# A two-layer token backbone on one core: lower parts of the output projection on GpSimd, an overflow flag computed behind the first gather, two weight splits behind the router's scores, and a later estimate of the experts' transfers

## The chip, the cores and the metric

The kernel runs on one core of one Trainium2 chip. The core has a matrix engine (TensorE, PE in the profile), a vector engine (VectorE, DVE), an activation engine (ScalarE, ACT), GpSimd (POOL), and SyncE (SP), which here issues most transfers. All weights lie in the chip's main memory and are brought in by DMA. The metric is device time in microseconds (us), lower is better. The kernel before has a median of 1495.08 us over three runs (1493.68 to 1499.86).

## The reference, cut to what matters

The input is 256 latent tokens of 1024 values and 256 context tokens. Two layers follow each other; each is a token mixer and then a mixture of experts, both added to the stream, and a last RMS norm. All arithmetic is float32.

```python
for i in range(2):
    hx = rmsnorm(x, mix_norm_g[i]) * (1 + sc1) + sh1
    yx = rglru_mixer(...) if i == 0 else sgu_mixer(...)   # ends in an output projection (... @ w_out)
    x = x + g1 * yx
    hx = rmsnorm(x, ffn_norm_g[i]) * (1 + sc2) + sh2
    x = x + g2 * moe_ffn(hx, ...)

def moe_ffn(xn, ...):
    scores = sigmoid(xn @ router_w)                       # 64 experts
    ... # 4 of 8 groups of experts are kept, then the top 8 experts of each token
    gate = chosen scores / their sum * 2.5
    # each chosen expert: (silu(x @ w_gu[:, :256]) * (x @ w_gu[:, 256:])) @ w_down, times its gate
    return routed + swiglu(xn, ws_gu, ws_down)            # and one shared expert for all tokens
```

Layer 0's mixer is a recurrent block: input projection, gates, a linear scan in both directions over five heads of 256, and the output projection `a_w_out` (1280 x 1024). Layer 1's is a gated MLP.

## The kernel before, in words

**Order of work.** The program writes the order of each engine's instructions by hand (a manual schedule): an engine does its instructions in the order in which the Python code issues them, and waits where an operand is not there yet. Layer 0's mixer takes the span from 0 to about 248 us, its experts to about 787, layer 1's mixer to about 948 and its experts to about 1487.

**Float32 by three products.** TensorE multiplies such operands in a shorter format, so a weight and an activation are each split in an upper part and a lower part, and `mm3` makes three products (upper by upper, upper by lower, lower by upper). Activations' parts are `zh`, `zl`, `hh`, `hl`, `fh`, `fl`; weights' are `wh`, `wl`. The weights are split by `splitter`: ScalarE casts a piece into `wh` (L564), and another engine subtracts it from the piece into `wl` (L565); which one, the caller's function `eng(i, c)` says for tile i and piece c. Calling the splitter's `get(q)` issues casts and subtractions up to two pieces ahead of piece q.

**Layer 0's mixer.** Its weight tiles of 1 MB are split in pieces of 128x1024 (two per tile). The output projection has four tiles O0 to O3 and a tile Q; they are multiplied while the last heads' scans run on VectorE. `split_eng` (L707) gives O0 to GpSimd, and of O1, O2 and O3 the first piece to GpSimd and the second to VectorE; Q's two pieces go to VectorE. `ready(n)` (L716) asks the splitter for pieces up to n; `B(h, q)`, the gates of head h, calls it once for each of its two halves jt (L838), ahead of the activations L841 and L842.

**Experts.** At the start of a layer's experts, `rstd_of` takes a root (ScalarE, L532) and VectorE's L533 to L535 finish it; the router's scores (L1270, a tanh L1271) follow, then the choice of experts on VectorE, counts on TensorE behind the mask `mb` (L1325), and a list `order` of the 64 experts by load (L1358). SyncE then starts their transfers, in that order. Each expert has three tiles of 1 MB: two of `m_gu` (gate and up) and one of `m_dn`. They stream through a ring of 12 slots (`wr`, `wx`); class `Stream` issues a tile's transfer (L382) when a slot has come free. Tokens are gathered by a product with a 0/1 matrix `S` (`gather`, bank `b<-S,xt`, into `xg`), multiplied by `gate_up` (GU, `b<-wr,xg` and `b<-wx,xg`), turned (`flip`), multiplied by `down` (DN, `b<-wr,ht`), and scattered back.

**Work that is always there.** The shared expert, two fixed experts and five of the heaviest ones are computed for all 256 tokens by `over_all` (steps of `s<-hh,wh`: here called up-steps, six products of 128x256 in a half step) and `all_down` (`b<-fh,wh`: down-steps, 24 products). They wait in a list `ups`; the planner places them. `up(n)` issues n of them; `until(tiles)` issues them as long as it believes that the next expert's tile has not arrived:

```python
st.now = st.dma = max(st.now, st.dma)                # L1361, when order is known
self.dma = max(self.dma, self.since.get(w, 0.0)) + LOAD   # LOAD, LATE = 2.6, -0.3
self.due.append(self.dma + LATE)                     # in pump(), for each transfer
if t <= st.now: break                                # until(): t is the tile's due time
```

`st.now` is the planner's own clock, moved on by fixed costs of each step. Before the root L532, `over_all` of the shared expert issues the splits of its first four pieces (the cast L564 on ScalarE, the subtraction on GpSimd); only then does `up(1)` return and `rstd_of` follow.

**Overflow flag.** A general path handles an input in which an expert gets more tokens than its slots. A flag says whether it is needed: `cape` and `over` on VectorE (L1418, L1420), a product of 1x1 on TensorE (L1423), a cast on VectorE (L1424). `overflow()` makes the engines load the flag (L1428) and branch; it stands after `gather(0, 0)` and `gather(0, 1)` in the program. In this data the path is not taken.

Of the kernel before, what the change touches and what calls it, by code (L numbers as in the profile page):

```python
# [10 lines left out]
F32 = mybir.dt.float32  # L11
F32R = mybir.dt.float32r
BF = mybir.dt.bfloat16
I32 = mybir.dt.int32
AF = mybir.ActivationFunctionType
OP = mybir.AluOpType

P = 128
# [211 lines left out]
LOAD, LATE = 2.6, -0.3  # L230
COST = dict(step=1.46, down2=2.95, half=3.6, side=0.6, scatter=4.0, flip=0.25, gather=2.0, down=3.6)
# [70 lines left out]
def _body(nc, tc, a, pp, rp, ps, ps1, dr):  # L302
    V, S, G, PE = nc.vector, nc.scalar, nc.gpsimd, nc.tensor
    st = Stream(nc)

    def mm(out, lhsT, rhs, start, stop):
        PE.matmul(out, lhsT, rhs, start=start, stop=stop, skip_group_check=True)  # L307
# [7 lines left out]
    def bank(shape=(P, 512)):  # L315
        return ps.tile(list(shape), F32, name="b")
# [321 lines left out]
    def mixer0(rx):  # L638
      with tc.tile_pool(name="m0", bufs=1) as mp, tc.tile_pool(name="m0t", bufs=2) as tp:
# [67 lines left out]
        def split_eng(i, c):  # L707
            kind, j = plan0[users[i]]
            return G if (kind, j) in (("A", 0), ("O", 0)) or kind == "O" and c == 0 else V
# [5 lines left out]
        def ready(n):  # L715

            wq(n - 3)
# [93 lines left out]
        def B(h, q):  # L811
# [4 lines left out]
            for jt in range(2):  # L816
# [21 lines left out]
                ready(q + 7 + jt)  # L838
# [310 lines left out]
    def moe(l, tail):  # L1149
      rsb = bank()  # L1150
      with tc.tile_pool(name=f"e{l}", bufs=1) as mp, tc.tile_pool(name=f"e{l}t", bufs=2) as tp:
# [33 lines left out]
        def lower(i, c):  # L1185
            return V if c % 2 else G

        def over_all(ns, gate=None, eng=None):

            wq = splitter(tp, ns, eng or lower, 5)  # L1190
            p, out, at = [], [], []
# [28 lines left out]
            ups.append((lambda: wq(-1 if eng is None else 1), ns[0], 0.0, None))  # L1220
# [37 lines left out]
        prev = (over_all(sgu, eng=lambda i, c: G if i == 0 else lower(i, c)), sdn)  # L1258
# [12 lines left out]
        S.activation(out=sc, in_=sc, func=AF.Tanh, scale=0.5)  # L1271
        spread()
# [88 lines left out]
        st.now = st.dma = max(st.now, st.dma)  # L1361
# [54 lines left out]

        cape = mp.tile([P, 1], F32, name="cape")
        V.scalar_tensor_tensor(out=junk[:, :64], in0=pb[:, :64], scalar=1.0, in1=C["cap"], op0=OP.mult, op1=OP.mult, accum_out=cape)  # L1418
        over = mp.tile([P, 1], F32, name="over")
        V.tensor_tensor(out=over, in0=nc_, in1=cape, op=OP.is_gt)  # L1420
        pf = bank()
        mm(pf[0:1, 0:1], over[0:64, :], onesf[0:64, 0:1], True, True)
        flag = mp.tile([1, 1], I32, name="flag")  # L1423
        V.tensor_copy(out=flag, in_=pf[0:1, 0:1])  # L1424

# [145 lines left out]
        def spend(what):  # L1571
            st.now += COST[what]

# [3 lines left out]
        spend("gather")  # L1577
        overflow()
# [89 lines left out]
```

## Time and profile before

| | us |
|---|---|
| median of three runs | 1495.08 (1493.68 to 1499.86) |
| the profiled execution's own time | 1495.63 |
| its span, first to last instruction | 1493.5 |
| PE busy | 1401.8 (94%) |
| DVE busy | 757.3 (51%) |
| ACT busy | 517.7 (35%) |
| POOL busy | 325.4 (22%) |

The mean granted TensorE clock over the span is 0.977. The chain that ended last is 49% PE, 23% issue, 5% POOL, 3% DVE and 1% ACT. Of the chip's transfers the span moved 514.85 MB, at a mean of 345 GB/s. A busy share is a mean over stretches with different limits, so the timeline of each stretch says more: there a row gives the start, the time, engine, line, operation, the tile written and the tiles read, how many instructions it sums up, and in brackets the engine's idle time ahead of it with the instruction that ended it.

### The profile page before, as it was taken

Reading aid. Unit: us, or ns where it says so; the run is one execution under the profiler, and the core shown is the slowest. Engines: PE = TensorE matmul, PEld = TensorE weight load, DVE = VectorE, ACT = ScalarE, POOL = GpSimd, SP = SyncE. Lnnn points to the kernel's source line nnn. Section 1 sums busy time; section 2 is a strip of 40 time slices with the busy share of each in tenths; the row PEclk is TensorE's granted clock in tenths of the full one; section 3 lists DMA queues with packets and bytes.
Section 4 is the critical chain, followed back from the end, with each engine's and each line's share of the span. In section 5 each row is a group of like instructions: output and inputs, shape, how many; then the busy total and the mean of one; then the engine's idle time right before and its main releaser. Section 6 shows DMA issues by size and latency. Waiting matters only on the chain.

```text
span 1493.5 us, 27187 instructions
## 1 busy us (share of the span) xinstructions
PE 1401.8 (94%) x10752; PEld 978.8 (66%) x10752; DVE 757.3 (51%) x1378; ACT 517.7 (35%) x874; POOL 325.4 (22%) x412
## 2 busy tenths in 40 slices
PE   6899997998989999999999999889899999999997
PEld 4677776646556575666657899656556667566664
DVE  6689996514254333334446786533425334343534
ACT  4777883311123122222325445511212222212222
POOL 1300033410222212212101441421303222211210
PEclk9999999999999999999999999999999999999999
DMA  9766695598999999999999744469798999999994
GB/s 375 310 267 246 240 384 206 205 380 329 378 384 376 421 420 420 421 419 420 420 418 379 273 169 159 153 235 402 319 390 323 417 419 421 420 420 420 421 421 188
DMA packets 77443, 514.85 MB, mean 345 GB/s; under 512 B 9856, under 2 KB 10240, under 8 KB 17024
## 3 DMA queue, kind: packets, MB, share of 16 engines
q1 hardware_dynamic: 74720, 508.91, 84.2%
q10 hardware_dynamic: 2592, 4.16, 0.9%
q8 instruction: 86, 1.41, 0.4%
q14 instruction: 45, 0.37, 0.1%
HBM read 511.99 MB, written 1.05 MB: 344 GB/s over the span
## 4 chain that ended last, share of the span: by engine, by line
PE 49%; issue 23%; POOL 5%; DVE 3%; ACT 1%; ACTq 0%; POOLq 0%; DVEq 0%
PE b L307 42%; PE s L307 7%; POOL wl L565 2%; POOL S L1396 2%; PE b L1532 1%; DVE wl L565 1%; DVE h L990 0%; POOL Y L1281 0%; ACT wh L564 0%; DVE v L1109 0%; POOL hl L1286 0%; DVE v L1046 0%; DVE xt L1411 0%; DVE u L998 0%; ACT Y L1282 0%
## 5 line engine op out<-in xcount | busy, mean ns | idle before, releaser
L307 PE MATMUL b<-wr,xg 128*32 128x512 f32 (+2 forms) x1464 | 292.8, 599 | 4.8 <-DMA wr<-in_m_gu 3.2
L565 POOL TENSOR_TENSOR wl<-wr,wh 128x512 fp32r<-128x512 f32 (+1 forms) x67 | 98.4, 1480 | 605.4 <-ACT wh L564 573.3
L307 PE MATMUL b<-wx,xg 128*32 128x512 f32 (+2 forms) x744 | 199.4, 599 | 3.3 <-DMA wx<-in_m_gu 3.3
L565 DVE TENSOR_TENSOR wl<-wr,wh 128x512 fp32r<-128x512 f32 (+1 forms) x155 | 146.4, 971 | 50.8 <-ACT wh L564 49.8
L564 ACT CAST wh<-wr 128x512 fp32r<-128x512 f32 (+1 forms) x222 | 143.1, 684 | 74.5 <-PE b L307 46.6
L1157 DVE SCALAR_TENSOR_TENSOR xT<-b,mod,xT 128x256 f32<-128x256 f32 x304 | 130.3, 478 | 74.2 <-PE b L307 68.3
L1525 DVE TENSOR_TENSOR h<-h,b 128x256 f32<-128x256 f32 x44 | 18.5, 420 | 274.3 <-ACT h L1524 274.3
L307 PEld LDWEIGHTS b<-wr,xg 128*32 128x32 f32 (+2 forms) x1464 | 79.1, 118 | 118.3 <-issue 103.7
L1524 ACT ACTIVATE h<-b 128x256 f32<-128x256 f32 x44 | 16.9, 384 | 396.4 <-PE b L307 396.4
L307 PE MATMUL s<-hh,wh 128*128 128x256 f32 x512 | 151.1, 295 | 2.4 <-ACT wh L564 2.4
L307 PE MATMUL b<-wr,ht 128*32 128x512 f32 (+2 forms) x752 | 146.8, 597 | 1.6 <-ACT ht L1534 1.6
L307 PE MATMUL s<-hh,wl 128*128 128x256 f32 x512 | 144.1, 281 | 1.8 <-POOL wl L565 1.7
L1548 DVE SCALAR_TENSOR_TENSOR Y<-b,gt,Y 128x512 fp32r<-128x512 f32 x88 | 65.9, 750 | 154.1 <-ACT Y L1547 154.1
L307 PE MATMUL s<-hl,wh 128*128 128x256 f32 x512 | 143.6, 280 | 0.0
L565 POOL TENSOR_TENSOR wl<-wx,wh 128x512 fp32r<-128x512 f32 (+1 forms) x48 | 69.0, 1455 | 327.3 <-ACT wh L564 260.4
L307 PEld LDWEIGHTS s<-hh,wh 128*128 128x128 f32 x512 | 97.1, 190 | 30.1 <-issue 26.7
L1547 ACT ACTIVATE Y<-b,gt 128x512 fp32r<-128x512 f32 x88 | 60.4, 688 | 142.0 <-PE b L307 135.7
L307 PE MATMUL b<-wx,ht 128*32 128x512 f32 (+2 forms) x352 | 103.2, 599 | 1.3 <-DMA wx<-in_m_dn 0.8
L307 PEld LDWEIGHTS s<-hh,wl 128*128 128x128 f32 x512 | 97.0, 190 | 2.4 <-POOL wl L565 2.1
L1396 POOL TENSOR_SCALAR S<-cst,agq 128x32 fp32r<-128x32 f32 (+3 forms) x208 | 84.1, 429 | 66.1 <-PE b L307 51.0
L307 PEld LDWEIGHTS s<-hl,wh 128*128 128x128 f32 x512 | 97.3, 190 | 0.4
L307 PEld LDWEIGHTS b<-wx,xg 128*32 128x32 f32 (+2 forms) x744 | 50.2, 117 | 70.9 <-issue 60.1
(283 smaller groups left out, 2806.8 us busy)
## 6 DMA issues: line engine op xcount, KB each, us to landing
wr<-in_m_gu SPq DMA_DIRECT2D x174, 1024.0 KB, 12.9
wx<-in_m_gu SPq DMA_DIRECT2D x82, 1024.0 KB, 11.9
wr<-in_m_dn SPq DMA_DIRECT2D x81, 1024.0 KB, 11.9
wx<-in_m_dn SPq DMA_DIRECT2D x41, 1024.0 KB, 11.1
wr<-in_ada_w SPq DMA_DIRECT2D x32, 1024.0 KB, 9.1
wr<-in_a_in SPq DMA_DIRECT2D x10, 1024.0 KB, 8.1
wr<-in_ada SPq DMA_DIRECT2D x8, 1024.0 KB, 12.2
wr<-in_ada_h SPq DMA_DIRECT2D x6, 1024.0 KB, 5.1
```

The costliest lines, as they stand in the source:

```text
L307: PE.matmul(out, lhsT, rhs, start=start, stop=stop, skip_group_check=True)
L564: S.copy(out=hi, in_=t)
L565: eng(i, c).tensor_tensor(out=lo, in0=t, in1=hi.bitcast(F32), op=OP.subtract)
L1157: V.scalar_tensor_tensor(out=xT[:, d, :], in0=y, scalar=mod[:, l, 5, d:d + 1], in1=xT[:, d, :], op0=OP.mult, op1=OP.add)
L1396: (G if b else V).tensor_scalar(out=s[:, tt, i * P + o:i * P + o + wd], in0=C["iota1"][:, j:j + wd], scalar1=agq[:, tt, q:q + 1], scalar2= ...
L1524: S.activation(out=h, in_=p[:, :256], func=AF.Silu)
L1525: V.tensor_tensor(out=h, in0=h, in1=p[:, 256:], op=OP.mult)
L1532: PE.transpose(p[:, k * P:(k + 1) * P], h[:, k * P:(k + 1) * P], ident)
L1547: S.activation(out=hi, in_=p, func=AF.Copy, scale=gts[g])
L1548: V.scalar_tensor_tensor(out=y[:, 1, 512 * c:512 * c + 512], in0=p, scalar=gts[g], in1=hi.bitcast(F32), op0=OP.mult, op1=OP.subtract)
```

## The change

Four edits, in all of which the same things are computed.

1. `split_eng` gives every piece of O0 to O3 to GpSimd; and for head 4's second half (jt = 1) `ready` asks for two pieces more, ahead of L841.
2. Of the four pieces of the shared expert that are split ahead of the root, two stay there; the other two are issued by `more()`, behind the scores' tanh.
3. When `order` is known the planner's estimate of the transfers' start is set `ORDER` = 4.0 us behind its clock.
4. The flag's four instructions are issued behind the two gathers, still ahead of `overflow()`.

Two lines come in at the top, so a line of the kernel after is 2 (from L706 on 2, from L1189 on 4, behind L1271 up to 11) higher than before.

```diff
@@ -228,6 +228,8 @@
 
 
 LOAD, LATE = 2.6, -0.3
+
+ORDER = 4.0
 COST = dict(step=1.46, down2=2.95, half=3.6, side=0.6, scatter=4.0, flip=0.25, gather=2.0, down=3.6)
 
 READY = 5.0
@@ -706,7 +708,7 @@
 
         def split_eng(i, c):
             kind, j = plan0[users[i]]
-            return G if (kind, j) in (("A", 0), ("O", 0)) or kind == "O" and c == 0 else V
+            return G if (kind, j) == ("A", 0) or kind == "O" else V
 
 
         base = 8
@@ -835,7 +837,7 @@
                         p = pg[2 * g + d]
                         S.activation(out=(ta, ti)[g][:, d, :], in_=p, func=AF.Tanh, scale=0.5, bias=(rb_, ib_)[g][:, d, ft:ft + 1])
 
-                ready(q + 7 + jt)
+                ready(q + 7 + (3 if jt and h == 4 else jt))
                 for d in range(2):
                     n1, n2 = nz[:, d, ft:ft + 1], nz2[:, d, ft:ft + 1]
                     S.activation(out=te[:, d, :], in_=ta[:, d, :], func=AF.Tanh, scale=n1, bias=n1)
@@ -1185,9 +1187,11 @@
         def lower(i, c):
             return V if c % 2 else G
 
-        def over_all(ns, gate=None, eng=None):
+        def over_all(ns, gate=None, eng=None, early=None):
 
             wq = splitter(tp, ns, eng or lower, 5)
+            if early is not None:
+                early.append(wq)
             p, out, at = [], [], []
 
             def step(k, x):
@@ -1217,7 +1221,7 @@
                 V.tensor_tensor(out=lo, in0=fv, in1=hi.bitcast(F32), op=OP.subtract)
                 out.extend((hi, lo))
 
-            ups.append((lambda: wq(-1 if eng is None else 1), ns[0], 0.0, None))
+            ups.append((lambda: wq(-1), ns[0], 0.0, None))
             ups.extend([(lambda k=k, x=x: step(k, x), ns[min(k + 2, 7) // 4], COST["step"] / 2, None) for k in range(8) for x in range(2)])
             return out, at
 
@@ -1255,7 +1259,12 @@
         ngu = [[st.reserve("n_gu") for _ in range(2)] for _ in range(NAT)]
         sdn = st.reserve("s_dn")
         ndn = [st.reserve("n_dn") for _ in range(NAT)]
-        prev = (over_all(sgu, eng=lambda i, c: G if i == 0 else lower(i, c)), sdn)
+        early = []
+        prev = (over_all(sgu, eng=lambda i, c: G if i == 0 else lower(i, c), early=early), sdn)
+
+        def more():
+            early[0](1)
+
         for e in range(NAT):
             f = over_all(ngu[e], ident[:, 64 + e:65 + e])
             all_down(*prev)
@@ -1269,6 +1278,7 @@
         for tt in range(2):
             V.scalar_tensor_tensor(out=sc[:, tt, :], in0=tail.rt[:, tt, :], scalar=rstd[:, tt:tt + 1], in1=tail.csh, op0=OP.mult, op1=OP.add)
         S.activation(out=sc, in_=sc, func=AF.Tanh, scale=0.5)
+        more()
         spread()
         if l:
             for i in range(2, 4):
@@ -1358,7 +1368,8 @@
         V.tensor_scalar(out=order, in0=po[0:1, 0:64], scalar1=float(64 * l), scalar2=None, op0=OP.add)
         orders[l] = order
         st.ready.add(("order", l))
-        st.now = st.dma = max(st.now, st.dma)
+        st.now = max(st.now, st.dma)
+        st.dma = st.now + ORDER
         st.pump()
         V.tensor_scalar(out=sc, in0=sc, scalar1=0.5, scalar2=0.5, op0=OP.mult, op1=OP.add)
         V.tensor_copy(out=nc_, in_=ncol)
@@ -1413,16 +1424,6 @@
         up(9)
         if l:
             ada_half_done(5, ada_p, tp, "hf", 1)
-
-        cape = mp.tile([P, 1], F32, name="cape")
-        V.scalar_tensor_tensor(out=junk[:, :64], in0=pb[:, :64], scalar=1.0, in1=C["cap"], op0=OP.mult, op1=OP.mult, accum_out=cape)
-        over = mp.tile([P, 1], F32, name="over")
-        V.tensor_tensor(out=over, in0=nc_, in1=cape, op=OP.is_gt)
-        pf = bank()
-        mm(pf[0:1, 0:1], over[0:64, :], onesf[0:64, 0:1], True, True)
-        flag = mp.tile([1, 1], I32, name="flag")
-        V.tensor_copy(out=flag, in_=pf[0:1, 0:1])
-
 
         def overflow():
             fv = nc.values_load(flag[0:1, 0:1], min_val=0, max_val=64)
@@ -1575,6 +1576,16 @@
         gather(0, 1)
         spend("gather")
         spend("gather")
+
+        cape = mp.tile([P, 1], F32, name="cape")
+        V.scalar_tensor_tensor(out=junk[:, :64], in0=pb[:, :64], scalar=1.0, in1=C["cap"], op0=OP.mult, op1=OP.mult, accum_out=cape)
+        over = mp.tile([P, 1], F32, name="over")
+        V.tensor_tensor(out=over, in0=nc_, in1=cape, op=OP.is_gt)
+        pf = bank()
+        mm(pf[0:1, 0:1], over[0:64, :], onesf[0:64, 0:1], True, True)
+        flag = mp.tile([1, 1], I32, name="flag")
+        V.tensor_copy(out=flag, in_=pf[0:1, 0:1])
+
         overflow()
         for b in range(NB):
             if b + 1 < NB:
```

On GpSimd, at the output projection of layer 0 (`wr6` is the slot of O0, `wr5` of O1, `wx0` of O2, `wx1` of O3), before:

```order
L565 TENSOR_TENSOR wl_1755<-wr6_1683,wh_1754 128x1024
L565 TENSOR_TENSOR wl_1827<-wr6_1683,wh_1826 128x1024
L565 TENSOR_TENSOR wl_1911<-wr5_1693,wh_1910 128x1024
L565 TENSOR_TENSOR wl_1982<-wx0_1766,wh_1981 128x1024
L565 TENSOR_TENSOR wl_2065<-wx1_1768,wh_2064 128x1024
L619 TENSOR_TENSOR hf_2195<-hf_2195 128x256
```

And after:

```order
L567 TENSOR_TENSOR wl_1755<-wr6_1683,wh_1754 128x1024
L567 TENSOR_TENSOR wl_1827<-wr6_1683,wh_1826 128x1024
L567 TENSOR_TENSOR wl_1875<-wr5_1693,wh_1874 128x1024
L567 TENSOR_TENSOR wl_1915<-wr5_1693,wh_1914 128x1024
L567 TENSOR_TENSOR wl_1982<-wx0_1766,wh_1981 128x1024
L567 TENSOR_TENSOR wl_1986<-wx0_1766,wh_1985 128x1024
L567 TENSOR_TENSOR wl_2065<-wx1_1768,wh_2064 128x1024
L567 TENSOR_TENSOR wl_2069<-wx1_1768,wh_2068 128x1024
L621 TENSOR_TENSOR hf_2195<-hf_2195 128x256
```

GpSimd has eight such subtractions in place of five, and VectorE three fewer.

On ScalarE, where a layer's experts begin, the root has two casts fewer ahead of it; they come behind the tanh. The same holds in both layers.

On TensorE at the first gather (`b<-S,xt`) of layer 0, before:

```order
L307 MATMUL s_2441<-hh_2286,wl_2630 128x256
L307 MATMUL b_2691<-onesf_78,over_2689 1x1
L307 MATMUL b_2696<-S_2565,xt_2564 128x256 x8
L307 MATMUL b_2706<-S_2565,xt_2564 128x256 x8
L307 MATMUL b_2716<-S_2565,xt_2564 128x256 x8
L307 MATMUL b_2726<-S_2565,xt_2564 128x256 x8
L1428 TENSOR_LOAD flag_2693
```

And after:

```order
L309 MATMUL s_2441<-hh_2286,wl_2630 128x256
L309 MATMUL b_2688<-S_2565,xt_2564 128x256 x8
L309 MATMUL b_2698<-S_2565,xt_2564 128x256 x8
L309 MATMUL b_2708<-S_2565,xt_2564 128x256 x8
L309 MATMUL b_2718<-S_2565,xt_2564 128x256 x8
L309 MATMUL b_2732<-onesf_78,over_2730 1x1
L1429 TENSOR_LOAD flag_2734
```

The gather's 32 products come first, and the flag's product stands next to the flag's load. On VectorE two of the copies into `xg` (L1474 before) are now ahead of `cape`.

On TensorE in the third batch of layer 0, where the shared expert's first down-steps (`b<-fh,wh`) begin, before:

```order
L307 MATMUL s_2925<-hh_2286,wh_3217 128x256
L307 MATMUL s_2925<-hl_2287,wh_3217 128x256
L307 MATMUL s_2925<-hh_2286,wl_3218 128x256
L307 MATMUL b_3357<-fh_2681,wh_3349 128x256
L307 MATMUL b_3357<-fl_2682,wh_3349 128x256
L307 MATMUL b_3357<-fh_2681,wl_3350 128x256
```

And after (`ST` and `Y` are a scatter's operands):

```order
L309 MATMUL b_3338<-ST_2884,Y_3088 128x256 x2
L309 MATMUL b_3338<-ST_3049,Y_3153 128x256 x2
L309 MATMUL b_3338<-ST_2884,Y_3088 128x256 x2
L309 MATMUL b_3338<-ST_3049,Y_3153 128x256 x2
L309 MATMUL b_3357<-fh_2681,wh_3349 128x256
L309 MATMUL b_3357<-fl_2682,wh_3349 128x256
L309 MATMUL b_3357<-fh_2681,wl_3350 128x256
```

Before, the down-steps followed an up-step directly; after, a scatter stands between. In the whole of a layer's experts before the fifth batch, the number of up-steps and down-steps on TensorE is the same in both programs, and their places differ; from the fifth batch on the two orders are the same. Of the three places of a layer in which a down-step directly follows an up-step, the first two are replaced by one (behind the third batch's second gate and up); the third stays.

## Rows read from the trace of the kernel before

**Rows 1.** Windows: start:end, length, busy by engine, granted clock, DMA share, GB/s.

```profile
275.00:295.00 20.00, 16.52 (x99) 10.82 (x101) 6.21 (x15) 4.58 (x9) 5.01 (x11) 1.00 0.53 202
345.00:360.00 15.00, 11.89 (x76) 8.58 (x77) 6.77 (x9) 2.70 (x5) 2.96 (x2) 0.77 0.57 212
465.00:765.00 300.00, 296.09 (x2366) 188.83 (x2369) 120.66 (x219) 73.03 (x135) 62.35 (x89) 0.99 1.01 420
1045.00:1060.00 15.00, 11.41 (x81) 8.23 (x80) 6.86 (x9) 3.30 (x6) 2.97 (x2) 0.89 0.53 202
```

**Rows 2.** Timeline of POOL, output projection of layer 0.

```profile
208.96 2.46 POOL L565 TENSOR_TENSOR wl<-wr,wh 128x1024 fp32r<-128x1024 f32 x1 [7.07 <-ACT wh L564]
216.25 5.63 POOL L565 TENSOR_TENSOR wl<-wx,wh 128x1024 fp32r<-128x1024 f32 x2 [4.83 <-ACT wh L564]
```

**Rows 3.** Timeline of DVE, the same stretch.

```profile
195.46 2.71 DVE L868 TENSOR_TENSOR_SCAN hf<-Tt,T,I 128x256 f32<-128x256 f32 x1
...
198.78 0.75 DVE L868 TENSOR_TENSOR_SCAN T<-Tt,T,I 128x256 f32<-128x256 f32 x1
...
214.40 1.22 DVE L565 TENSOR_TENSOR wl<-wr,wh 128x1024 fp32r<-128x1024 f32 x1
...
232.66 3.49 DVE L565 TENSOR_TENSOR wl<-wx,wh 128x1024 fp32r<-128x1024 f32 x3
```

**Rows 4.** Timeline of PE, the same stretch.

```profile
233.93 0.39 PE L307 MATMUL b<-zh,wl 128*128 128x256 f32 x1 [2.55 <-DVE wl L565]
```

**Rows 5.** Timelines of ACT, POOL, DVE and SP, root to first expert transfer, layer 0.

```profile
248.97 2.18 ACT L564 CAST wh<-wx 128x512 fp32r<-128x512 f32 x4 [1.82 <-PE s L307]
...
249.67 5.00 POOL L565 TENSOR_TENSOR wl<-wx,wh 128x512 fp32r<-128x512 f32 x4 [3.54 <-ACT wh L564]
...
252.24 1.20 DVE L534 TENSOR_TENSOR rs_m<-rs_m,rq_y 128x2 f32<-128x2 f32 x1
...
267.18 0.95 SPq L382 DMA_DIRECT2D wr<-in_m_gu  x2
```

**Rows 6.** Timeline of PE, first gather of layer 0 and of layer 1.

```profile
280.63 0.18 PE L307 MATMUL b<-onesf,over 64*1 64x1 f32 x2 [2.65 <-DVE over L1420]
280.75 4.10 PE L307 MATMUL b<-S,xt 128*128 128x256 f32 x32
285.67 4.53 PE L307 MATMUL b<-wr,xg 128*128 128x512 f32 x10 [0.83 <-DVEq L1429]
...
980.69 0.19 PE L307 MATMUL b<-onesf,over 64*1 64x1 f32 x2 [3.25 <-DVE over L1420]
980.80 5.58 PE L307 MATMUL b<-S,xt 128*128 128x256 f32 x32
```

**Rows 7.** Timelines of DVE and POOL at the flag, layer 0.

```profile
280.86 0.15 DVE L1424 CAST flag<-b 1x1 int32<-1x1 f32 x1 [0.37 <-PE b L307]
...
282.01 2.11 POOL L1396 TENSOR_SCALAR S<-cst,agq 128x64 fp32r<-128x64 f32 x5 [7.47 <-DVE flag L1424]
```

**Rows 8.** Timeline of PE, experts of layer 0, and the waits on one releaser.

```profile
304.36 1.05 PE L307 MATMUL b<-wx,xg 128*32 128x512 f32 x2 [1.27 <-DMA wx<-in_m_gu]
...
347.55 0.58 PE L307 MATMUL b<-fh,wh 128*128 128x256 f32 x1 [2.74 <-ACT wh L564]
...
349.49 0.41 PE L307 MATMUL b<-fl,wh 128*128 128x256 f32 x1
349.71 0.41 PE L307 MATMUL b<-fh,wl 128*128 128x256 f32 x1
...
421.13 0.38 PE L307 MATMUL b<-fh,wh 128*128 128x256 f32 x1 [3.08 <-ACT wh L564]
...
PE b L307 <- ACT wh L564: 17.6, 7, 3.1
```

**Rows 9.** Timelines of SP and PE, end of layer 1's experts.

```profile
1458.79 2.72 SPq L382 DMA_DIRECT2D wx<-in_m_dn  x2
...
1475.05 0.63 PE L307 MATMUL b<-wr,ht 128*32 128x512 f32 x3 [0.52 <-ACT ht L1534]
```


## The prediction, made before the changed kernel was run

> **What bounds the kernel now.** I read the windows first, stage by stage. In the middle of layer 0's experts, 465 to 765 us, the transfers run at 420 GB/s, a DMA share of 1.01, and PE is busy 296.09 of 300 us [rows 1]: both are full, so nothing is won there by moving instructions. Layer 1 is alike. Earlier in the same stage the transfers have holes: share 0.53 in 275 to 295, 0.57 in 345 to 360, and 0.53 in 1045 to 1060 of layer 1 [rows 1]. Against 1.01 that is 20 x 0.48 = 9.6 us, 15 x 0.44 = 6.6 us and 15 x 0.48 = 7.2 us of transfers not made. All tiles pass through one ring in a fixed order, so an experts' stage lasts about as long as its full-rate transfers plus these holes, after the first transfer (267.18 in layer 0, [rows 5]). The end confirms it: SyncE issues the last loads in a row that starts at 1458.79, and PE's last DN starts at 1475.05 [rows 9], little more than a tile's way behind. Then I read what stands at the holes in the timelines of PE, ACT, POOL and DVE, and the aggregated waits. An edit counts if it starts the transfers earlier, or lets PE free a slot earlier where a hole is.
>
> **The output projection.** VectorE loses three subtractions of 1.22 us [rows 3], 3.6 us in all; GpSimd gains three of about 2.46 [rows 2]. PE's wait of 2.55 us for VectorE's `wl` of O3 [rows 4] goes: GpSimd's two pieces start at 216.25 and take 5.63, so four would be done near 228, ahead of 231.4, where PE now starts to wait (233.93 less 2.55). But the price of GpSimd's work is paid on VectorE: the scan L868, which reads two tensors, takes 2.71 us beside a GpSimd subtraction and 0.75 without one [rows 3], so about 2.0 us is lost for each subtraction that meets such an operation. Three more of them cost up to 6.0; against 3.6 saved, VectorE's list is 2.4 us later, and its last item, Q's split, ends now at 232.66 + 3.49 = 236.15 and then near 238.5. PE now has O3's second part from 233.93 ahead of Q, 24 products at some 0.17 us each (5.58/32, a gather at a lowered clock, [rows 6]), and comes to Q at 238.1, about 2 us behind that split. With Q's split at 238.5 only some 0.4 us of the 2.4 would show, and a further part where other operations are held a little longer than these; I let 1 us show, with the saved wait of 2.55 turned into one for Q. O1's first cast, issued one step earlier on ScalarE, costs L841 one cast and is hidden by the wait of VectorE's list for itself. Bounds: if the new subtractions meet nothing, the wait and a little of VectorE's time are won, -3; if one more scan is held (2.0) on top and PE drops to the lower clock for the wait, as it does at 349.49 [rows 8], +4.6. I take +1.
>
> The Trainium skill (GPSIMD Engine Reference, section 1, Specifications) says that GpSimd shares its memory interfaces with VectorE and contends with Vector instructions that have two inputs. The trace agrees: 2.71 against 0.75 us. By that rule applied to every new subtraction the term would be at its upper bound, +4.6, and this is the third rival's mechanism.
>
> **The root and the scores.** Four casts take 2.18 us ahead of the root [rows 5], two would take 1.09: the root comes 1.1 us earlier. GpSimd's four subtractions take 5.00, to 254.67; L534, an operation on 128x2, takes 1.20 beside them [rows 5], and with GpSimd done at 252.2 up to 1 us more is saved on L534 and L535. The two moved subtractions then meet later operations of the router that read two tensors, and give part back. From 2.1 gained I keep 1.3 for each layer. Bounds 0 (all is given back) and -2.1. The moved casts' reader, an up-step, stands behind `mb` in PE's order, which hides them. The first transfer hangs on the end of this chain, so this shifts the whole stage: -2.6 in both layers (0 to -4.2).
>
> **The flag.** In layer 0 PE waits 2.65 us for `over`, then makes the gather's 32 products in 4.10 us, and starts GU at 285.67 after another 0.83; in layer 1 it waits 3.25 us and the gather takes 5.58 at a lowered clock [rows 6]. After the change the gather follows the up-steps without that wait. But the flag's load now stands behind it: the second copy into `xg` and the two small operations of VectorE, the product, the cast, then what POOL shows between the cast's end at 281.01 and its next instruction at 282.01 [rows 7], 1.0 us. VectorE's copy, `cape` and `over` end, by my estimate, 0.5 us behind the gather, since the second copy needs only the third of its four banks; with the product of 0.18 and the cast of 0.15 [rows 6, 7] and the 1.0 that is 1.8 in place of 0.83. So layer 0 wins 2.65 - 1.0 = 1.7, layer 1 3.25 + (5.58 - 4.10) - 1.0 = 3.7, less 0.4 because I do not trust the whole clock gain: 3.3. Does anything else wait there? SyncE's next load waits for GU to free a slot, not for the flag; and this is inside the 9.6 us hole, so GU's shift counts in full. Sum -5.0. Bounds: all of both waits and the clock, -6.5; a load of the flag that is 2 us slower behind PE's queue in each layer than I put it, and a clock that falls all the same, +1.
>
> **The planner.** By the later estimate `until` puts more up-steps ahead of the second and third waits; the count is equal by the fifth batch. Where VectorE, ScalarE and PE hand a shared expert over (last up-step, silu, product, cast, down-step), PE stands 2.74 us at 347.55 and 3.08 at 421.13; seven waits of this form cost 17.6 us in both layers [rows 8]. At 347.55 a scatter now covers the hand-over. What follows also gains: from 349.49 products come 0.22 us apart [rows 8], against 4.10/32 = 0.128 at full clock [rows 6], 24 x 0.09 = 2.1 us. So 2.74 + 2.1 = 4.8 on PE, in the 6.6 us hole; in layer 1 its like lies in the 7.2 us hole. At 421.13 the direct hand-over goes too, but a new one comes behind the third batch, so I count it as 0. The wait of 1.27 for a tile at 304.36 [rows 8] is filled with an up-step, and the up-steps placed first instead of second delay the first GU by 0.7: again 0 in sum. Other holes stay. I take -5 for each layer, -10. Bounds: 0, if the ring's next limit is met at once; -12 for each, if both hand-overs and the waits for tiles all go.
>
> **Sum.** +1 - 2.6 - 5.0 - 10 = -16.6 on the profiled execution's own 1495.63 (span 1493.5 and 2.1 around it, which stays): 1479.0. The median of the runs shown is 0.55 below that execution, less than any term, and I leave the sum as it is.
>
> **Rivals.**
> First, the planner's gain is taken back: transfers start and end by the ring, and the new hand-over in the third batch, of 2.74 to 3.08 us with its lowered clock, stands where the DMA share is just filling up. For it: PE is 98.7% busy from 465 on, so lost time there is not made good. Against it: the 345 to 360 hole is real and its cause is removed. Then +1 - 2.6 - 5.0 = -6.6: 1489.0.
> Second, all holes behind the hand-overs close: -12 for each layer and the rest as forecast, less 4 for what the last DN needs behind the last transfer: +1 - 2.6 - 5.0 - 24 + 4 = -26.6: 1469.0. For it: seven waits, 17.6 us. Against: three or so of these remain in the order.
> Third, slower: GpSimd's subtractions hold VectorE. Its place is the output projection, +4.6, and the router's operations with two inputs, +0.4 in each layer instead of -1.3; it decides if the flag and the planner together give less than 5.4. With those two at zero the sum is +5.4: 1501.0. For it: 2.71 against 0.75 us [rows 3]. Against: two waits seen in the trace would have to stay with their causes gone.
> Fourth, the change does not do what it says: the flag's chain behind the gather is as long as the one ahead of it, and the planner's order is worth nothing in the ring; then +1 - 2.6 = -1.6: 1494.0.
>
> **Chances.** Forecast 0.58 (its own range 1473 to 1486), first rival 0.21, second 0.07, third 0.07, fourth 0.07. The range 1467 to 1492 takes in the first two rivals and leaves out the last two and parts of the others' tails, about 0.2. About 0.5%, 7.5 us, is what a measurement of this kernel can tell from no change: faster is below 1487.6, slower above 1502.6. The forecast, the second rival and a third of the first give faster, 0.58 + 0.07 + 0.07 = 0.72; the rest of the first, the fourth and most of the third are the same, 0.23; slower 0.05, the third's upper part.
>
> **What would show it.** Right: the first expert transfer of each layer about 1 to 2 us earlier, measured from the stage's start; GU right behind a gather without the waits of 2.65 and 3.25; no wait of 2.74 ahead of the first down-step and a DMA share of 0.8 or more where 345 to 360 has 0.57; Q's split near 238.5. Wrong: an idle PE between gather and GU of over 3 us (flag term); holes of the same total in other windows (planner term); Q starting 3 us later or earlier than now (output projection).

## The result, and the profile after

The kernel after has a median of 1472.41 us over four runs (1469.22 to 1475.43), the kernel before, beside it, 1494.82. The ratio is 0.9843 with an interval of [0.9808, 0.9879]: 22 us faster by the medians, 23.5 by the ratio. The forecast was 1479.0, in a range of 1467 to 1492, with a chance of 0.72 for faster; the result lies just below the forecast's own range, 1473 to 1486. The profiled execution took 1469.6 us, its span 1467.7; so the traces differ by 25.8 us of span, more than the medians, and a profile must not be read to the last microsecond: before the output projection, where both programs do the same, the trace of after is already 2.5 us ahead.

From the windows of the trace of after (start:end, length, busy time and count by engine, granted clock, DMA share, GB/s), first the answers to [rows 1], then layer 1 in stretches of 20 us that begin 80, 160 and 180 us behind its first expert transfer:

```profile
275.00:295.00 20.00, 16.55 (x75) 10.42 (x79) 6.26 (x13) 5.36 (x10) 6.53 (x12) 0.89 0.48 186
345.00:360.00 15.00, 15.00 (x148) 9.54 (x147) 4.87 (x12) 1.38 (x3) 1.30 (x1) 1.00 0.98 392
465.00:765.00 300.00, 294.60 (x2394) 185.30 (x2396) 118.64 (x219) 69.95 (x131) 61.00 (x88) 0.99 1.01 420
1045.00:1060.00 15.00, 15.00 (x115) 9.65 (x113) 5.30 (x8) 5.06 (x9) 6.40 (x12) 1.00 1.01 422
...
1033.21:1053.21 20.00, 20.00 (x175) 12.01 (x174) 6.47 (x13) 3.77 (x8) 0.00 (x0) 1.00 0.95 384
1113.21:1133.21 20.00, 19.14 (x153) 13.71 (x152) 10.38 (x22) 3.95 (x8) 3.84 (x3) 1.00 0.98 395
1133.21:1153.21 20.00, 20.00 (x174) 14.73 (x173) 4.36 (x8) 4.65 (x9) 1.30 (x1) 1.00 1.00 409
```

The same three stretches of layer 1 in the trace of before, 80, 160 and 180 us behind its first transfer (964.49):

```profile
1044.49:1064.49 20.00, 16.41 (x125) 10.72 (x127) 8.52 (x13) 3.30 (x6) 2.97 (x2) 0.91 0.64 254
1124.49:1144.49 20.00, 20.00 (x131) 11.65 (x130) 7.03 (x16) 3.49 (x7) 5.41 (x12) 0.89 0.78 312
1144.49:1164.49 20.00, 20.00 (x175) 15.21 (x177) 10.12 (x20) 3.97 (x7) 5.25 (x5) 1.00 0.84 338
```

The hole at 80 us closes, as forecast (0.64 to 0.95), but so do the holes at 160 and 180 us (0.78 and 0.84 to 0.98 and 1.00), of which the forecast had counted nothing ("Other holes stay"). The first hole, 275 to 295 us, does not close (0.53 to 0.48). Adding length x (1.01 - share) over the first 240 us of a stage gives the transfers not made: 29 us in layer 0 and 35 in layer 1 before, 23 and 21 after.

The rows of after for the flag [rows 6, 7] and the hand-over [rows 8], from the timeline of PE and the aggregated waits (us in total, times, longest):

```profile
276.27 3.99 PE L309 MATMUL b<-S,xt 128*128 128x256 f32 x32
280.52 0.18 PE L309 MATMUL b<-onesf,over 64*1 64x1 f32 x2 [0.26 <-DVE over L1583]
282.45 4.09 PE L309 MATMUL b<-wr,xg 128*128 128x512 f32 x6 [1.75 <-DVEq L1430]
...
396.63 0.58 PE L309 MATMUL b<-fh,wh 128*128 128x256 f32 x1 [2.74 <-ACT wh L566]
...
PE b L309 <- ACT wh L566: 11.7, 5, 2.7
```

The gather stands right behind the up-steps, without the wait of 2.65 us for `over`; the wait of 1.75 ahead of the first gate and up has taken the place of 0.83. Five hand-overs that wait for ScalarE's cast are left of seven, 11.7 us of 17.6. The one at 347.55 is gone, a new one stands at 396.63.

The rows of after for the output projection and the root [rows 2 to 5], DVE, POOL, PE, ACT and SP:

```profile
215.03 2.76 DVE L867 TENSOR_TENSOR_SCAN T<-Tt,I 128x256 f32<-128x256 f32 x1
217.83 2.70 DVE L870 TENSOR_TENSOR_SCAN hf<-Tt,T,I 128x256 f32<-128x256 f32 x1
...
233.79 2.35 DVE L567 TENSOR_TENSOR wl<-wx,wh 128x1024 fp32r<-128x1024 f32 x2
...
214.89 7.83 POOL L567 TENSOR_TENSOR wl<-wx,wh 128x1024 fp32r<-128x1024 f32 x3 [4.30 <-ACT wh L566]
...
232.49 0.41 PE L309 MATMUL b<-zh,wh 128*128 128x256 f32 x1 [3.80 <-DVE zh L909]
233.12 0.58 PE L309 MATMUL b<-zl,wh 128*128 128x256 f32 x1 [0.22 <-DVE zl L910]
235.06 0.58 PE L309 MATMUL b<-zh,wl 128*128 128x256 f32 x1 [1.36 <-DVE wl L567]
...
247.97 1.14 ACT L566 CAST wh<-wx 128x512 fp32r<-128x512 f32 x2 [1.82 <-PE s L309]
...
265.06 2.13 SPq L384 DMA_DIRECT2D wr<-in_m_gu  x3
```

VectorE's scans take 2.7 us beside the row of GpSimd subtractions, and PE, which no longer waits 2.55 us for O3's `wl`, waits 3.80 for VectorE's next result in its place (`zh`). Q's split ends at 233.79 + 2.35 = 236.14, as before (236.15), though the stretch began 2.5 us earlier. PE has done O3 by then, so its waits of 3.80, 0.22 and 1.36 us all stand ahead of Q, and it makes Q's products at the lower clock. Windows of after, then of before, at Q:

```profile
235.00:239.00 4.00, 3.81 (x16) 3.52 (x17) 2.15 (x5) 0.39 (x1) 0.00 (x0) 0.50 0.44 131
```

```profile
238.00:241.00 3.00, 3.00 (x27) 3.00 (x27) 0.88 (x2) 0.70 (x2) 0.00 (x0) 0.97 0.84 350
```

### The profile page after: what moved, and what is told of

The parts are those of the page before. It is cut to its first block, busy times and chain, and to the rows that moved or that the text cites. A ratio compares the mean times of both kernels' runs of the same rounds, so it can differ in the third digit from the quotient of the medians.

```text
span 1467.7 us, 27203 instructions
## 1 busy us (share of the span) xinstructions
PE 1392.4 (95%) x10752; PEld 973.3 (66%) x10752; DVE 753.6 (51%) x1375; ACT 518.7 (35%) x874; POOL 331.8 (23%) x415
## 5 line engine op out<-in xcount | busy, mean ns | idle before, releaser
L309 PE MATMUL b<-wr,xg 128*32 128x512 f32 (+2 forms) x1464 | 306.5, 600 | 4.6 <-DMA wr<-in_m_gu 2.9
L567 POOL TENSOR_TENSOR wl<-wr,wh 128x512 fp32r<-128x512 f32 (+1 forms) x82 | 121.2, 1492 | 704.5 <-ACT wh L566 654.5
L309 PE MATMUL b<-wx,xg 128*32 128x512 f32 (+2 forms) x744 | 234.3, 598 | 1.7 <-SPq L1430 1.4
L566 ACT CAST wh<-wr 128x512 fp32r<-128x512 f32 (+1 forms) x230 | 147.4, 682 | 84.5 <-PE b L309 44.8
L309 PEld LDWEIGHTS b<-wr,xg 128*32 128x32 f32 (+2 forms) x1464 | 83.9, 118 | 134.9 <-issue 119.5
L309 PE MATMUL b<-wr,ht 128*32 128x512 f32 (+2 forms) x712 | 141.9, 596 | 1.5 <-ACT ht L1535 1.5
L309 PEld LDWEIGHTS s<-hh,wh 128*128 128x128 f32 x512 | 98.2, 192 | 28.7 <-issue 25.3
L309 PE MATMUL b<-wx,ht 128*32 128x512 f32 (+2 forms) x392 | 109.1, 595 | 0.5 <-ACT ht L1535 0.5
L567 POOL TENSOR_TENSOR wl<-wx,wh 128x512 fp32r<-128x512 f32 (+1 forms) x36 | 53.6, 1506 | 199.2 <-ACT wh L566 192.6
L309 PE MATMUL b<-S,xt 128*128 128x256 f32 x704 | 94.5, 287 | 0.0
## 6 DMA issues: line engine op xcount, KB each, us to landing
wr<-in_m_gu SPq DMA_DIRECT2D x167, 1024.0 KB, 12.7
```

The costliest lines, as they stand in the source:

```text
L566: S.copy(out=hi, in_=t)
L567: eng(i, c).tensor_tensor(out=lo, in0=t, in1=hi.bitcast(F32), op=OP.subtract)
```

## The experiments

Twelve kernels ran, one of them the kernel after again. Times are medians; a difference in us is the ratio's distance from 1 times the median of before in the same group (1495.3 or 1496.0), with its interval.

**One edit alone, in the kernel before.** The flag's block moved:

```diff
         gather(0, 1)
         ...
+        cape = ...; over = ...; mm(pf[0:1, 0:1], over, onesf); flag = ...
         overflow()
```

> The kernel before with only the flag's block moved behind the first gather. Theory (each part acts by itself): the first gate-and-up product starts 1.5 us earlier behind the up-steps in layer 0 and 3.5 us in layer 1, as between the two traces; the whole is 4 to 6 us faster. Rival 1 (the excess over the forecast belongs to the flag: an earlier start of the products also closes later holes of the transfers): 10 to 13 us faster. Rival 2 (the ring takes it back): within 1 us of before.

Measured: 1489.83 us, 0.9974 [0.996, 0.9987], that is -3.9 us [-6.0, -1.9]. From the first transfer to the first gate and up the trace has 16.85 us in layer 0 (18.49 before), and from the root to it 33.3 in layer 1 (36.7). The timeline of PE, layer 0:

```profile
278.08 4.00 PE L307 MATMUL b<-S,xt 128*128 128x256 f32 x32
282.32 0.18 PE L307 MATMUL b<-onesf,over 64*1 64x1 f32 x2 [0.25 <-DVE over L1572]
284.29 1.96 PE L307 MATMUL b<-wr,xg 128*128 128x512 f32 x4 [1.78 <-DVEq L1419]
```

The first theory holds, the excess over the forecast is not the flag's.

The planner's estimate alone:

```diff
-        st.now = st.dma = max(st.now, st.dma)
+        st.now = max(st.now, st.dma)
+        st.dma = st.now + ORDER                      # ORDER = 4.0
```

> The kernel before with only ORDER = 4.0. Theory: the order of up-steps alone brings the 8.0 and 9.7 us that the two traces differ by behind the first product of each layer, 15 to 19 us faster. Rival 1: 9 to 11 us faster, as forecast, and the rest belongs to the flag's move. Rival 2: with the flag's wait still there the later up-steps meet other tiles, and less than 5 us is left.

Measured: 1476.80 us, 0.9884 [0.9866, 0.9902], -17.3 us [-20.0, -14.7]. In its trace the stretch from the first gate and up of layer 0 to the root of layer 1 is 654.8 us long (664.7 before, 655.0 after), and the holes of the first 240 us are 22 and 23 us (29 and 35 before). The first theory holds: this one number is most of the change, and the forecast of -10 was too small by three quarters.

The two splits behind the tanh alone:

```diff
-            ups.append((lambda: wq(-1 if eng is None else 1), ns[0], 0.0, None))
+            ups.append((lambda: wq(-1), ns[0], 0.0, None))   # and early[0](1) behind the tanh
```

> The kernel before with only two of the four early splits put behind the scores' tanh. Theory: in layer 0 the first transfer comes 1.1 us earlier from the stage's start; in layer 1 TensorE stands still longer ahead of the mask (4.1 us in place of 1.6), its clock falls, the 18 up-step products ahead of the list take 0.21 us each in place of 0.12, and the first transfer comes 0.6 us later; in sum 0 to 1 us faster. Rival (the forecast: 1.3 us in each layer, and the layer-1 clock in the trace of after was an accident): 2 to 3 us faster, products at 0.12 us there.

Measured: 1494.50 us, 0.9996 [0.9983, 1.0009], -0.6 us [-2.5, +1.3]. Between root and mask the trace has 9.07 us in place of 9.14, so what is won is the root's own 1.0 us. In layer 1 the time from the mask to the first transfer is 6.7 us, 4.7 in the trace of before; but it is 6.1 to 6.3 in the three traces of one edit alone that don't have this one (flag, planner, output projection), so most of that difference is not the edit's: the trace of before was the odd one. My first theory had the right sum and in layer 1 mostly the wrong cause.

The output projection alone:

```diff
-            return G if (kind, j) in (("A", 0), ("O", 0)) or kind == "O" and c == 0 else V
+            return G if (kind, j) == ("A", 0) or kind == "O" else V
-                ready(q + 7 + jt)
+                ready(q + 7 + (3 if jt and h == 4 else jt))
```

> The kernel before with only the lower parts of the output projection on GpSimd and the earlier cast. Theory: Vector operations with two inputs are held 2 us by each new subtraction, six more are saved 3.6: Q's split and the mixer's end come 1 to 2.5 us later, so 1 to 2.5 us slower. Rival 1: no effect on the end, within 0.5 us, since TensorE no longer waits 2.55 us for O3. Rival 2: 2 us faster (the trace of after reaches the root of layer 0 1.0 us earlier than before, and the 2.5 us of head start that it has ahead of the output projection would be due to the change).

Measured: 1499.48 us, 1.0026 [1.0012, 1.0040], +3.9 us [+1.8, +6.0]: this edit makes the kernel slower. The timeline of DVE:

```profile
216.53 2.75 DVE L865 TENSOR_TENSOR_SCAN T<-Tt,I 128x256 f32<-128x256 f32 x1
219.31 2.68 DVE L868 TENSOR_TENSOR_SCAN hf<-Tt,T,I 128x256 f32<-128x256 f32 x1
221.92 2.82 DVE L865 TENSOR_TENSOR_SCAN T<-Tt,I 128x256 f32<-128x256 f32 x1
224.77 2.71 DVE L868 TENSOR_TENSOR_SCAN T<-Tt,T,I 128x256 f32<-128x256 f32 x1
```

Four scans in a row, 2 us more each than the 0.7 us that they take alone [rows 3]. In its trace Q's split comes 2.5 us later from the start of the stretch than in before, and the end of the mixer 2.3 us later (1.5 in the trace of after).

**The output projection in the kernel after.** All lower parts on VectorE (the earlier cast stays):

```diff
-            return G if (kind, j) == ("A", 0) or kind == "O" else V
+            return G if (kind, j) == ("A", 0) else V
```

> The kernel after with all eight lower parts of O0 to O3 on VectorE and none on GpSimd (the earlier cast stays). Theory (GpSimd's subtractions hold Vector operations with two inputs for about 2 us each): no scan takes 2.7 us any more; VectorE makes eight subtractions of 1.2 us and is held by none, so its list from O's start to Q's split is 8 x 2.0 - 8 x 1.2 = about 6 us shorter than in the kernel after, and TensorE, then the bound there, ends the mixer 3 to 5 us earlier: 0.2 to 0.35% faster than the kernel after, 1.8 to 1.9% faster than before. Rival (VectorE's own load is the limit, and the held operations only look long): 8 x 1.2 us more on VectorE, the mixer ends 2 to 5 us later than in the kernel after.

Measured: 1467.06 us, 0.9800 [0.9779, 0.9821]. The same two scans as above, then PE:

```profile
215.13 0.69 DVE L867 TENSOR_TENSOR_SCAN T<-Tt,I 128x256 f32<-128x256 f32 x1 [0.46 <-ACT wh L566]
215.86 0.75 DVE L870 TENSOR_TENSOR_SCAN hf<-Tt,T,I 128x256 f32<-128x256 f32 x1
...
229.25 0.58 PE L309 MATMUL b<-zh,wl 128*128 128x256 f32 x1 [3.68 <-DVE wl L567]
```

With GpSimd idle nothing is held: 0.69 and 0.75 us in place of 2.76 and 2.70, with the same operands. VectorE's list ends at 232.60. Both programs do the same up to the pair of splits on VectorE ahead of the projection (from 184.94 here, from 183.75 in after); counted from there the list ends 4.7 us earlier than in after, not 6. PE still waits 3.68 us, now for O3's `wl`, which stands behind `zh` and `zl` on VectorE. That GpSimd holds VectorE is shown, and the fourteen traces count it: between 190 and 236 us as many VectorE operations take 2.4 us or more as GpSimd makes subtractions, five, eight or none. The size of the gain on VectorE was forecast too high.

The edit undone:

```diff
-            return G if (kind, j) == ("A", 0) or kind == "O" else V
+            return G if (kind, j) in (("A", 0), ("O", 0)) or kind == "O" and c == 0 else V
-                ready(q + 7 + (3 if jt and h == 4 else jt))
+                ready(q + 7 + jt)
```

> The kernel after with the output projection's edit undone (split and cast as before). Theory (the edit alone costs 4 us timed, 2.5 in its trace): 2 to 4 us faster than the kernel after. Rival (in company of the other edits the edit is free, since the mixer's later end is hidden in the transfers of the next stage): same as the kernel after within 1 us, and the first expert transfer as early from the start of the output projection.

Measured: 1467.97 us, 0.9812 [0.9789, 0.9836]: 4 us faster than the kernel after, the same price as alone. For this kernel by itself that is at the edge of the noise; with the kernels before and behind it, all three without the extra work on GpSimd and 3 to 5 us below the kernel after, the rival (hidden in the next stage) falls.

All on VectorE and the cast where it was:

```diff
-            return G if (kind, j) == ("A", 0) or kind == "O" else V
+            return G if (kind, j) == ("A", 0) else V
-                ready(q + 7 + (3 if jt and h == 4 else jt))
+                ready(q + 7 + jt)
```

> The kernel after with all lower parts of O0 to O3 on VectorE and the cast where it was before the change. Theory (the edit's price is VectorE held by GpSimd, and without GpSimd there it is gone; then TensorE bounds the projection): as fast as the kernels with the edit undone or with all on VectorE, 1464 to 1469, and 3 to 6 us faster than the kernel after in the same group. Rival (the earlier cast was what helped on VectorE): 2 to 4 us slower than the kernel with all on VectorE and the earlier cast.

Measured: 1469.15 us, 0.9812 [0.9789, 0.9834]. With the two kernels above it lies within some 2 us; whether the cast's place counts can't be told from this.

**The planner's number in the kernel after.** `ORDER = 2.0`:

> The kernel after with ORDER = 2.0: up-steps move forward by 6 to 12 products, but the last up-step of the shared expert again stands directly ahead of its first down-step, as in the kernel before. Theory (the gain of the planner comes from the removed hand-over, its lowered clock and the hole of the transfers that they cause): the wait of 2.7 us and the hole 80 to 90 us behind the first transfer are there again, and 5 to 9 us of the planner's 17 are lost in both layers together. Rival (it comes from the earlier up-steps and the later holes, not from that hand-over): within 3 us of the kernel after.

Measured: 1478.08 us, 0.9886 [0.9862, 0.9910], 6 us slower than the kernel after. Windows 80 to 100 us behind its first transfer, layer 0, then PE and the waits:

```profile
345.67:365.67 20.00, 19.14 (x165) 13.31 (x166) 8.53 (x15) 4.13 (x9) 5.56 (x4) 0.91 0.70 254
...
345.26 0.38 PE L309 MATMUL b<-fh,wh 128*128 128x256 f32 x1 [2.74 <-ACT wh L566]
...
PE b L309 <- ACT wh L566: 14.1, 7, 2.7
```

The hand-over and its hole (0.70) are back, and from the first gate and up to the root of layer 1 it takes 659.1 us in place of 655.0. From its first transfer to the end of its last DN a layer takes 504.8 and 502.2 us here, 501.7 and 499.7 in after, 510.8 and 514.2 in before (the first two with the flag's move). So 4.0 in place of 2.0, with the removed hand-over in it, is worth some 3 us in a layer, and two thirds of the planner's 17 us are there while the hand-over still stands. They come with the up-steps that lie further ahead: the holes at 160 and 180 us are about half closed (shares 0.95 and 0.89 in layer 0, 0.88 and 0.97 in layer 1; before 0.90, 0.81, 0.78 and 0.84).

`ORDER = 6.0` (output projection as before the change):

> The kernel after without the output projection's edit, with ORDER = 6.0: 18 more up-step products ahead of the second wait, and two uncovered hand-overs per layer early in the stage in place of one. Theory (holes decide: each uncovered hand-over costs about 4 us while the ring is not yet full, and up-steps put too early make the first hole longer): 6 to 12 us slower than with ORDER = 4.0. Rival (the earlier the up-steps the better): 2 to 6 us faster.

Measured: 1495.93 us, 0.9995 [0.9978, 1.0011]: all that the change brought is gone, 28 us against the same kernel with 4.0. PE and the waits:

```profile
328.86 0.39 PE L309 MATMUL b<-fh,wh 128*128 128x256 f32 x1 [2.74 <-ACT wh L566]
...
386.32 0.38 PE L309 MATMUL b<-fh,wh 128*128 128x256 f32 x1 [2.74 <-ACT wh L566]
...
PE b L309 <- ACT wh L566: 25.9, 11, 3.1
```

Eleven hand-overs are uncovered, 25.9 us, and the holes of the first 240 us are 35 and 33 us (29 and 35 in the kernel before). The theory had the direction, and less than half of the size.

**TensorE's clock ahead of the list of experts.** Small products without use, whose results nobody reads, between the rstd's transposes and the mask:

```diff
+        keep(onesb, 20)                               # 20 of 128x128
         ...
+        keep(gs.rearrange("p t g -> p (t g)"), 6)     # 6 behind gs, 8 behind kp
```

> The kernel after with 34 small products without use on TensorE in each layer, between the rstd's transposes and the mask, where it otherwise stands still 4.1 to 4.4 us (results unread). Theory (standing still lowers the clock, and the 18 up-step products ahead of the list of experts then take 0.213 us in place of 0.117): the products take 0.12 us again, and the first transfer of each layer comes 1.5 to 1.7 us earlier behind the mask; 2 to 3.5 us faster than the kernel after. Rival (the clock falls whatever small products stand there, or the products delay the mask's own): the up-step products stay at 0.2 us and the time is the same or up to 2 us longer.

Measured: 1475.05 us, 0.9857 [0.9836, 0.9879], not faster than the kernel after (the profiled execution took 1481.12 us). First a row of after (layer 1, behind an idle PE of 4.10 us), then of this kernel (layer 0):

```profile
947.30 0.19 PE L309 MATMUL b<-onesb,mb 128*128 128x1 bf16 x2 [4.10 <-issue]
...
947.95 0.41 PE L309 MATMUL s<-hl,wh 128*128 128x256 f32 x1
948.16 0.41 PE L309 MATMUL s<-hh,wl 128*128 128x256 f32 x1
```

```profile
259.35 0.28 PE L309 MATMUL s<-hl,wh 128*128 128x256 f32 x1
259.47 0.28 PE L309 MATMUL s<-hh,wl 128*128 128x256 f32 x1
...
272.51 0.38 PE L309 MATMUL s<-hl,wh 128*128 128x256 f32 x1 [1.34 <-DVE hl L1296]
...
311.81 0.89 PE L309 MATMUL b<-wr,xg 128*32 128x512 f32 x3 [2.74 <-DMA wr<-in_m_gu]
```

The clock stays up: starts 0.12 us apart in place of 0.21, and from mask to first transfer 5.3 us in place of 7.0 in layer 0. But PE, faster now, waits 1.34 us for `hl` from VectorE, and later 2.74 for a tile; from the first transfer to the gather it takes 14.0 us in place of 11.2. The first half of the theory holds, and the gain is given back a few us later. Two traces show the same without such products: with `ORDER` = 6.0 and with all on VectorE and the cast where it was, PE stood still only 2.2 us ahead of the mask in layer 0 and 5.7 us pass from mask to first transfer, but PE then waits 2.6 us for `hl`.

**The kernel after once more**, and **a hand-over taken out where the transfers are full**:

> The kernel after itself, timed once more beside the kernels of this group, since its four runs fell in two clusters (1469 and 1475). Theory (the four edits act each by itself): their sum from the runs alone is -3.9 - 17.3 - 0.6 + 3.9 = -18, so about 1.2% faster than before, some 1477. Rival (the trace's -25.8 and the first median are right, and the edits help one another): 1.6 to 1.7% faster, 1469 to 1471.

Measured: 1471.79 us, 0.9839 [0.9818, 0.9861], -24.1 us [-27.2, -20.8].

```diff
-READY = 5.0
+READY = 7.0    # in the kernel after with the output projection's edit undone
```

`READY` is the time that the planner allows from an expert's last up-step to its first down-step.

> The kernel after without the output projection's edit, with READY = 7.0: in each layer the last direct hand-over (at 613.61 in the trace of after, 2.74 and 0.77 us and a lowered clock behind it) gets a gate and up in between; nothing ahead of it moves. Theory (where the transfers run at a share of 1.01 TensorE's waits cost nothing): the wait goes and the time stays, within 1.5 us of the same kernel with READY = 5.0. Rival (TensorE, 98% busy there, is as much the bound): 4 to 8 us faster.

Measured: 1462.61 us, 0.9778 [0.9752, 0.9804], 5 us faster than with 5.0. The runs alone put that at the edge of the noise; the traces say the same, and my theory falls. From PE and SP of the kernel with 5.0, then with 7.0. The SP line is the last expert transfer of layer 0, whose first is issued at 263.72 and 266.66; the last line of each is the last DN of layer 1, whose first transfers are issued at 948.84 and 948.77:

```profile
609.44 0.39 PE L309 MATMUL b<-fh,wh 128*128 128x256 f32 x1 [2.74 <-ACT wh L566]
610.79 0.39 PE L309 MATMUL b<-fh,wl 128*128 128x256 f32 x1 [0.76 <-POOL wl L567]
...
744.05 0.33 SPq L384 DMA_DIRECT2D wr<-in_m_dn  x1
...
1447.51 3.64 PE L309 MATMUL b<-wr,ht 128*32 128x512 f32 x32 [0.52 <-ACT ht L1535]
```

```profile
611.48 0.62 PE L309 MATMUL b<-wr,xg 128*32 128x512 f32 x2 [0.77 <-DMA wr<-in_m_gu]
...
747.09 0.33 SPq L384 DMA_DIRECT2D wx<-in_m_dn  x1
...
1440.88 3.90 PE L309 MATMUL b<-wr,ht 128*32 128x512 f32 x32 [0.52 <-ACT ht L1535]
```

In place of the waits PE does products and then meets a tile that is not there yet (0.77). The transfers get no faster by it: in layer 0 the last is issued 480.3 and 480.4 us behind the first and lands 12.7 and 12.9 us later. What gets shorter is the work that PE still has then: the last DN ends 5.8 us behind that landing with 5.0 and 2.4 with 7.0 (layer 1: 6.2 and 2.4). So PE, 98% busy, does not make a wait good before the stage ends, though the transfers lose nothing. From the first transfer to the start of the last DN, layer 1 takes 498.7 and 492.1 us; some 2.5 of that difference comes from transfers ahead of the changed place. This kernel has the lowest median of all, 9 us below the kernel after.

## Why the prediction was right, and where it was not

The direction and the range were right. The sum was -16.6, and the runs give -23.5 [-28.7, -18.1] and, once more, -24.1 [-27.2, -20.8]. That the four edits alone add up to -18, near the sum, is partly luck: three terms were taken too favourably by 6 us together, and the planner too low by 7.

- **Flag, -5.0.** Right in size and in each of its parts: -1.6 and -3.4 us in the trace of the edit alone (1.7 and 3.3 forecast), -3.9 [-6.0, -1.9] in the runs; the load of the flag puts GU 1.75 us behind its product, and from the gather's end to GU it takes 2.2 us, 1.8 forecast.
- **Output projection, +1.** The mechanism was right, the sign too, and Q's split came where it was put: 2.5 us later from the start of the stretch, 2.4 forecast. What was mis-sized is how much of it shows, +3.9 [+1.8, +6.0] and not 1. I set the saved wait of 2.55 us against it, but the held scans make `zh` late too: PE waits 3.80 us for it, 5.4 us in all ahead of Q, and then makes Q's products at a granted clock of 0.50 (1.2 of 2.4 GHz), where in before it came to Q straight from O3 and had 0.97. The lower clock stood in my upper bound alone, and that bound, +4.6, was nearer than my value. The Trainium skill (GPSIMD Engine Reference, section 1, Specifications) says that GpSimd shares its memory interfaces with VectorE and contends with its instructions that have two inputs there. The trace agrees, 2.70 us beside GpSimd and 0.75 without it.
- **Root and scores, -2.6.** Too large: -0.6 [-2.5, +1.3]. In layer 0 of the trace of after, the root comes 1.0 us earlier and the scores, behind it, 1.25 us more, but 1.2 of it is lost by the mask beside the two moved subtractions; 1.1 is left. In layer 1 the root comes 1.0 us earlier too, and the first transfer is 0.6 us later in the trace of after, because TensorE was at the full clock there (products 0.12 us apart) in the trace of before and in no other trace without the small products. Against the three traces of one other edit the first transfer of layer 1 comes 0.9 to 1.1 us earlier. So the traces give the edit 1 us in each layer; the runs can't tell this from nothing.
- **Planner, -10.** This is the term that was mis-sized most: -17.3 [-20.0, -14.7]. I gave all of it to the removed hand-over, 5 us in a layer; by the kernel with 2.0 it is worth some 3. The steps "again 0 in sum" and "Other holes stay" failed: the larger part comes from the up-steps that moved ahead, and the holes at 160 and 180 us closed as well. That PE reached the later tiles earlier is the likely reason; no run shows it by itself. The new hand-over at 396.63 did not take the gain back, as the first rival had it: the DMA share stays at 1.01 around it (385 to 405 us) and falls only in the next 20 us, to 0.80.
- **The rivals.** The result lies nearer to the second (1469.0, chance 0.07) than to the forecast (1479.0), and what the windows show is in part its mechanism, that the holes behind the hand-overs close.
- **The bound.** "Nothing is won there by moving instructions" (465 to 765 us) was wrong, though the change did not touch it: a wait of 2.74 us on PE in that stretch, taken out in each layer, gives 5 us in both together. The DMA share is at 1.01 all the while; most of the gain comes behind the last transfer.

The four edits alone add up to -18 us, the whole is -24; without the output projection the other three add up to -22 and are -28 [-31.6, -24.5] together. So they help one another by some 6 us, little more than the error of that sum; where, the runs do not settle.

## What to carry to other kernels

Where a stream of weights and an engine are both near full, list the holes of the whole stage before pricing an edit that moves work forward: later holes can close with the first. An uncovered hand-over of some 5 us (wait and lowered clock) cost 2 to 3 us in a layer where the transfers ran at full share, and with 6.0, early in the stage, six more of them came with 28 us. Look also at what the engine still has to do when the last tile lands. Price work given to GpSimd by what VectorE does beside it, not by VectorE's freed time. A planner's constant that seems to be an estimate is an order in disguise: 2 and 4 us here gave 1478 and 1472, and 4 and 6, with the projection undone, 1468 and 1496.

## What the runs showed that was not expected

- PE at the lower clock after some 4 us of standing still (granted 0.50 in 258 to 262 us of after) takes 0.213 us for a product in place of 0.117; in the chain to the list of experts 18 such products cost 1.7 us. Keeping PE busy there holds the clock, and in the kernel that does it nothing of this reaches the end.
- Between the fourteen profiled executions the same code reached VectorE's last splits ahead of the output projection at 183.0 to 186.5 us; differences below 3.5 us are only to be read from runs, or from one place to the next of the same trace.
